# A DRAM scratch tensor laid out by token chunk instead of by channel tile, in a hybrid flow-matching step

## The chip, the cores and the metric

The kernel runs on one core of a Trainium2 chip. The metric is the device time of one execution in microseconds (us); the time of a kernel is the median of three executions. Engines are called as in the profile: PE is the matrix engine (its weight loads are PEld), DVE the vector engine, ACT the scalar engine, POOL the GpSimd engine, SP the sync engine, which here only starts DMA transfers. SPq, ACTq and POOLq are the same engines' DMA issues. On-chip memory has 128 partitions; PE writes into PSUM banks, and an engine that copies a result out of such a bank is said here to evict it.

## The reference

One layer of a network on two token groups, 2,048 sample tokens and 128 prompt tokens. The part that the change touches is the first token mixer, a gated DeltaNet: queries, keys and values come from one projection, pass a short convolution over the tokens, and are then used in 128-token chunks.

```python
proj = jnp.einsum('btd,de->bte', xn, w_in)
qkv, beta, dec, z_a, u_b, v_b, z_b, x_c, z_c, gates = jnp.split(proj, points, axis=-1)
qkv = short_conv(qkv, conv_w).astype(jnp.float32)        # 3 taps over the tokens, then SiLU
q, k, v = jnp.split(qkv, 3, axis=-1)                     # 4 heads of 128 channels each
q = l2norm(q.reshape(B, T, H_A, DK)) * (DK ** -0.5)
k = l2norm(k.reshape(B, T, H_A, DK))
o, s_f, s_b = delta_bidir(q, k, v, g, beta, s0_f, s0_b)  # chunked scan, forward and backward
o_a = (rmsnorm(o, o_norm_g) * jax.nn.silu(z_a)).reshape(B, T, W_BR)
o_b = chunk_sgu(u_b, v_b, sgu_norm_g, w_spatial, b_spatial) * jax.nn.silu(z_b)
o_c = fourier_mix(x_c, grid) * jax.nn.silu(z_c)
pb = jnp.einsum('btnw,nwd->btnd', jnp.stack([o_a, o_b, o_c], axis=2), w_branch)
merged = jnp.einsum('btnd,btnd->btd', jax.nn.sigmoid(gates), pb)
out = jnp.einsum('btd,de->bte', merged, w_out)
```

## The kernel before

Tokens stand as 17 chunks of 128: chunks 0 to 15 are the sample, chunk 16 the prompt. Every product is done in three half-precision passes (`xh`/`xl` and `whi`/`wlo` are high and low parts), so one 128-channel tile of a projection over 512 tokens is 24 matmuls.

The stages, in the order of PE's work: normalise and transpose the input, with the projection of the first gate (to about 160 us of the profile); the convolution stage (to about 430 us); the v projection of the second mixer with its spatial mixing (17 blocks of 128 tokens, to about 560 us); the rest of the second mixer, the Fourier mixer, the merges and the output projection.

The convolution stage is a loop over 12 channel tiles `ct`: tiles 0 to 3 are the four heads of q, 4 to 7 those of k, 8 to 11 those of v. For each, PE computes five token blocks (four of 512, one of 128) into PSUM banks, ACT evicts each into `raw` (L646), DVE makes the three taps into `y`, the tile `cy` (L649 to L651), ACT and POOL apply SiLU (L654, L655), POOL starts the store of the whole row to the DRAM scratch `qkvD` (L656, 128 partitions with 8.7 KB runs), and ACT takes sums of squares of q and v (L658). `raw` and `cy` have two buffers each. PSUM banks for this loop alternate between a group of three (`ps_mm`) and another three (`ps_d`).

At the end of the stage the on-chip memory of the loop (`a1p`) is given to the next tiles: the first load into it is `bsp`, the biases of the spatial mixing (L1172), and ACT's sums of squares of the v projection (L1209) write there too. So both wait for the last store of `cy`.

From there on, a second strand of work runs beside the projections: `delta()`, a Python generator that `pace.tick` and `pace.part` advance while the projections are written down, so that its instructions fall between the matmuls. Its first part, `prep`, goes over the chunks in the order 16, 0, 1, ... 15. For each it takes the four-head tiles of k, v and q from `qkvD` with `rows` (L688; tiles `kq` with three buffers for k and v, `qr` with two for q), turns them on PE (L717), normalises, splits, multiplies, and stores what the scan needs through ACT's queue (L699) and POOL's (L746, L775). After each group of four chunks, `base_inverse` loads `nd` (L804), solves on DVE (L814, L815) and hands its result `ei` to ACT's queue (two stores, L704). The scan over chunks begins at about 890 us.

SP issues nearly all loads, in one queue, in program order: weight blocks `wst` (L227), the chunk loads, the decay rows `dc` (L790), and, for the second mixer, four rows `vrow` of `vsD` (L1228, L1234), which L1240 on DVE uses. What stands in that queue behind an issue that waits, waits too. The framework's scheduler fixes the order on every engine before the run, from its own estimates of when things are ready; at run time each engine follows that order and waits on semaphores.

Of the kernel before, what the change touches and what calls it, by code (L numbers as in the profile page):

```python
# [14 lines left out]
AF = mybir.ActivationFunctionType  # L15
# [5 lines left out]
P = 128  # L21
D = 1024
KT = 8
NS = 2048
NP = 128
NTOK = NS + NP
NCH = NTOK // P
H = 4
# [10 lines left out]
TBS = [(0, 512), (512, 512), (1024, 512), (1536, 512), (2048, 128)]  # L39
# [104 lines left out]
def hybrid_flow_kernel(ctx: ExitStack, tc: tile.TileContext, x_prompt, x_sample, state_delta, c, c_ctx, ln_g, w_ada,  # L144
# [3 lines left out]
    V, A, G, PE, SY = nc.vector, nc.scalar, nc.gpsimd, nc.tensor, nc.sync  # L148
# [9 lines left out]
    def sb(pl, shape, tag, dt=F32, bufs=None):  # L158
        kw = {} if bufs is None else {"bufs": bufs}
        return pl.tile(list(shape), dt, tag=tag, name=nm(tag), **kw)  # L160
# [11 lines left out]
    def bank(pl, shape, tag="b"):  # L172
        if pl is ps_d:
            rot[0] += 1
            pl = ps_d[rot[0] % 3]
        return pl.tile(list(shape), F32, tag=tag, name=nm(tag))

    def dram(name, shape, dt=F32):
        return drp.tile(list(shape), dt, tag=name, name=name)
# [82 lines left out]
    def gemm_T(ps, w, c0, rh, rl, nkt=KT, start=True, stop=True):  # L262
        for k in range(nkt):
            mm(ps, w.hi[:, k, c0:c0 + P], rh[:, k, :], start and k == 0, False)
            mm(ps, w.hi[:, k, c0:c0 + P], rl[:, k, :], False, False)
            mm(ps, w.lo[:, k, c0:c0 + P], rh[:, k, :], False, stop and k == nkt - 1)
            if k % 2:
                pace.part(rh.shape[-1] / 400)
# [52 lines left out]
    def getw(n=1, ahead=0):  # L321
        i = wnext[0]
        wnext[0] += n
        fetch(i + n)
        while len(wdone) - len(wsteps) < i + n:
            weight_step()
        fetch(i + n + ahead)
        r = wdone[i:i + n]
        return r[0] if n == 1 else r
# [89 lines left out]
    for blk in range(8):  # L419
# [3 lines left out]
        ps = bank(ps_d, [2, 256])  # L423
# [41 lines left out]
    for ti, (t0, tn) in enumerate(TBS):  # L465
# [13 lines left out]
        for k in range(KT):  # L479
            ps = bank(ps_d, [P, tn])  # L480
            for j in range(nt):
                PE.transpose(ps[:, j * P:(j + 1) * P], xt[:, j, k * P:(k + 1) * P], ident)
            t = sb(p0p, [P, tn], "xm", bufs=3)
# [3 lines left out]
        for g in range(4):  # L487
            ps = bank(ps_d if tn == P and g % 2 else ps_mm, [P, tn])
# [15 lines left out]
    LP = NTOK + 4  # L504
# [4 lines left out]
    rq = sb(dp, [P, NCH, H], "rq")  # L509
    vqs = sb(dp, [P, 12], "vqs")  # L510
    decD = [dram(f"dec{t}", [P, 2, WB]) for t in range(NCH)]
    qkvD = dram("qkv", [12, P, LP - 2])
    dl = ExitStack()
    dq = pool(dl, "dqa", 1, side="right")
    cfs = ExitStack()
# [112 lines left out]
        flush(*last)  # L628
        yield 1

    flip = [0]
    pace.start(decays(), 1.2)
    for ct in range(12):
        w = getw(1, 2 if ct < 6 else min(4, 15 - ct))
        for half in range(1):
            raw = sb(a1p, [P, LP], "raw")
            G.memset(raw[:, 0:1], 0.0)
            G.memset(raw[:, NS + 1:NS + 3], 0.0)
            G.memset(raw[:, LP - 1:LP], 0.0)
            for t0, tn in TBS:  # L640
                flip[0] ^= 1
                ps = bank(ps_d if flip[0] else ps_mm, [P, tn])
                gemm_T(ps, w, 0, xh[:, :, t0:t0 + tn], xl[:, :, t0:t0 + tn])
                o = t0 + 1 if t0 < NS else t0 + 3
                with tc.high_priority():
                    A.activation(raw[:, o:o + tn], ps, AF.Copy, scale=w.inv)  # L646
                pace.tick(tn / 100)
            y = sb(a1p, [P, LP - 2], "cy")
            V.tensor_scalar(y, raw[:, 0:LP - 2], convw(0, ct), None, ALU.mult)  # L649
            V.scalar_tensor_tensor(y, raw[:, 1:LP - 1], convw(1, ct), y, ALU.mult, ALU.add)  # L650
            V.scalar_tensor_tensor(y, raw[:, 2:LP], convw(2, ct), y, ALU.mult, ALU.add)  # L651
            for c0 in range(0, LP - 2, CQ):
                c1 = min(c0 + CQ, LP - 2)
                A.activation(raw[:, 1 + c0:1 + c1], y[:, c0:c1], AF.Sigmoid)  # L654
                G.tensor_tensor(y[:, c0:c1], y[:, c0:c1], raw[:, 1 + c0:1 + c1], ALU.mult)  # L655
            G.dma_start(qkvD[ct], y)  # L656
            if ct < 4 or ct > 7:
                A.activation(raw[:, 1:LP - 1], y, AF.Square, accum_out=vqs[:, ct:ct + 1])  # L658
    wsn = sb(ep, [P, WB], "st", bufs=3).rearrange("p (g q) -> p g q", g=4)
    SY.dma_start(wsn, w_spatial[0].rearrange("g p q -> p g q"))  # L660
    pace.drain()
    a1.close()


# [10 lines left out]
    eD = [dram(f"ei{g}", [2, 32, len(ts), H * 512], F16) for g, ts in enumerate(GROUPS)]  # L675
    hs = lambda h: slice(h * P, (h + 1) * P)

    def chunk_off(t):
        return t * P if t < 16 else NS + 2

    def bc(col, n):
        return col.rearrange("p (h o) -> p h o", o=1).to_broadcast([P, H, n])

# [1 line left out]

    def rows(part, t):
        x = sb(d2, [P, H, P], "kq" if part else "qr", bufs=3 if part else 2)
        SY.dma_start(x, qkvD[part * 4:part * 4 + 4, :, chunk_off(t):chunk_off(t) + P].rearrange("h p t -> p h t"))  # L688
        return x

    owed = []
# [16 lines left out]
    def prep(g, ci, t, nxt, held):  # L708
# [18 lines left out]
        def more(key, make):  # L727
            if nxt is not None:
                held[key] = make()

        more(1, lambda: rows(1, nxt))
        ps = turned(1)
        norm(ps, 1)
        V.tensor_tensor(h3(tok[:, 0, :]), h3(ps), bc(ss[:, 1, :], P), ALU.mult)
        yield 1
        more(0, lambda: rows(0, nxt))
        A.activation(tok[:, 1, :], turned(2), AF.Copy, scale=us)
        norm(turned(0), 0)
# [12 lines left out]
        made = A.activation(T[:, 0, :], ps, AF.Copy, scale=FS)  # L751
        V.scalar_tensor_tensor(T[:, 1, :], ps, FS, T[:, 0, :], ALU.mult, ALU.subtract)
        more(2, lambda: rows(2, nxt))
        late([(kTD[t], T)], made)
        yield 1
# [419 lines left out]
    ps = bank(ps_x, [P, 4, P])  # L1175
# [21 lines left out]
    for t in range(NCH):  # L1197
        ps = bank(ps_mm, [P, 4, P])
# [10 lines left out]
        made = A.activation(sq, vn.rearrange("p i c -> p (i c)"), AF.Square, accum_out=ss)  # L1209
# [19 lines left out]
    for g in range(4):  # L1229
# [5 lines left out]
        for ti, (t0, tn) in enumerate(TBS):  # L1235
            st = vrow[:, t0:t0 + tn]
            ps = bank(ps_mm, [P, tn])
# [26 lines left out]
    for g in range(4):  # L1264
        xw, zw = getw(2, 2)
        for gh in range(1):
# [20 lines left out]
            for q in range(0, NCH, 4):  # L1287
                qn = min(4, NCH - q)
                ps = bank(ps_mm, [P, qn, P])
                for i in range(qn):  # L1290
                    t = q + i
# [43 lines left out]
            for q4 in range(5):  # L1335
# [8 lines left out]
                if q4 == 2:  # L1344
                    ps = bank(ps_x, [P, P])
# [182 lines left out]
    part = sb(op, [P, 3], "part", bufs=1)  # L1528
    for i_, t in enumerate(order):
# [11 lines left out]
        for i, (c0, c1) in enumerate([(0, 512), (512, 896), (896, D)] if end else [(0, 512), (512, D)]):  # L1541
            cs = slice(c0, c1)
            ps = bank(ps_mm, [P, c1 - c0])
            gemm_N(ps, mh, ml, wo, c0, c1 - c0)
            dst, gc = (hh[:, cs], gt[:, cs]) if i_ else (gp[i], gp[i])
# [52 lines left out]
```

## Time and profile before

| | us |
|---|---|
| median of three executions | 2189.1 (2187.15 to 2190.76) |
| the profiled execution's own time | 2196.42 |
| its span | 2194.6 |
| PE busy in the span | 2125.6 (97%) |
| granted PE clock | 0.99 of full speed |

The profile shows one execution. The span runs from the first to the last instruction; 1.8 us lie around it. A group's row gives the line, engine, operation and tiles, its busy time and the idle time of its engine ahead of it. In a timeline the columns are the start in us, the duration in us, the engine, the line and the operation, and in square brackets the idle time ahead and what ended it. A row of DMA issues ends with the KB of each transfer and the median us from its issue to its landing.

### The profile page before, as it was taken

Reading aid. Unit: us, or ns where it says so; the run is one execution under the profiler, and the core shown is the slowest. Engines: PE = TensorE matmul, PEld = TensorE weight load, DVE = VectorE, ACT = ScalarE, POOL = GpSimd, SP = SyncE. Lnnn points to the kernel's source line nnn. Section 1 sums busy time; section 2 is a strip of 40 time slices with the busy share of each in tenths; the row PEclk is TensorE's granted clock in tenths of the full one; section 3 lists DMA queues with packets and bytes.
Section 4 is the critical chain, followed back from the end, with each engine's and each line's share of the span. In section 5 each row is a group of like instructions: output and inputs, shape, how many; then the busy total and the mean of one; then the engine's idle time right before and its main releaser. Section 6 shows DMA issues by size and latency. Waiting matters only on the chain.

```text
span 2194.6 us, 42626 instructions
## 1 busy us (share of the span) xinstructions
PE 2125.6 (97%) x16258; PEld 1220.6 (56%) x16258; DVE 1311.4 (60%) x3141; ACT 1014.4 (46%) x2345; POOL 734.8 (33%) x893
## 2 busy tenths in 40 slices
PE   7999999999999999899899999999999999999998
PEld 3564444455555577777555555555655444444444
DVE  5736854479868697466665555665664544233454
ACT  3535644455555574444644445655553422222332
POOL 1421533223334332442322233345542222212543
PEclk9999999999999999999999999999999999999999
DMA  8424733176776653444655556766664534333542
GB/s 282 152 87 161 257 109 110 60 215 211 250 225 226 213 168 106 119 126 140 214 162 162 167 166 187 229 196 213 212 194 148 166 131 130 109 102 109 183 150 106
DMA packets 233240, 365.11 MB, mean 166 GB/s; under 512 B 38369, under 2 KB 132938, under 8 KB 230986
## 3 DMA queue, kind: packets, MB, share of 16 engines
q1 hardware_dynamic: 180650, 267.38, 39.3%
q0 software_dynamic: 12688, 51.27, 6.4%
q10 hardware_dynamic: 39696, 43.72, 5.9%
q8 instruction: 128, 2.10, 0.4%
q14 instruction: 78, 0.64, 0.1%
HBM read 234.67 MB, written 127.62 MB: 165 GB/s over the span
## 4 chain that ended last, share of the span: by engine, by line
PE 46%; DVE 7%; DMA 6%; ACT 3%; issue 2%; POOL 1%; ACTq 0%; SPq 0%; POOLq 0%; DVEq 0%
PE b L193 46%; DMA st<-br 1%; DMA wst<-in_w_blk_dram 1%; DVE XB L814 1%; DVE E L815 1%; DMA ei<-XB 1%; DMA wst<-in_w_brb_dram 1%; DVE big L1376 1%; DVE wlo L251 0%; DMA ES<-ei 0%; ACT nd L767 0%; ACT big L1375 0%; DVE sv L1002 0%; DMA of<-sz 0%; DVE o L947 0%
## 5 line engine op out<-in xcount | busy, mean ns | idle before, releaser
L193 PE MATMUL b<-xh,whi 128*128 128x512 f16 (+1 forms) x1920 | 651.4, 348 | 7.2 <-DVE sg L1152 3.7
L193 PE MATMUL b<-xl,whi 128*128 128x512 f16 (+1 forms) x1920 | 651.6, 348 | 0.0
L193 PE MATMUL b<-xh,wlo 128*128 128x512 f16 (+1 forms) x1920 | 650.6, 348 | 0.0
L193 PEld LDWEIGHTS <-whi 128*128 128x128 f16 x3904 | 357.2, 98 | 338.5 <-issue 15.1
L193 PEld LDWEIGHTS <-wlo 128*128 128x128 f16 x1952 | 191.4, 98 | 178.0 <-issue 2.1
L193 PE MATMUL b<-big,bhi 128*128 128x512 f16 (+1 forms) x960 | 251.6, 347 | 4.2 <-ACT big L1375 3.6
L1415 POOL TENSOR_TENSOR mrow<-mrow,sg 128x512 f32<-128x512 f32 (+1 forms) x80 | 94.4, 1181 | 289.8 <-DVE sg L1414 164.6
L193 PE MATMUL b<-big,blo 128*128 128x512 f16 (+1 forms) x480 | 163.4, 347 | 0.0
L1405 ACT ACTIVATE sg<-b,winv 128x512 f32<-128x512 f32 (+1 forms) x120 | 74.2, 618 | 162.0 <-PE b L193 161.6
L193 PEld LDWEIGHTS <-xh 128*128 128x128 f16 x1496 | 118.7, 99 | 35.0 <-DVE yT L1328 4.0
L655 POOL TENSOR_TENSOR cy<-cy,raw 128x545 f32<-128x545 f32 (+1 forms) x48 | 74.9, 1587 | 182.0 <-ACT raw L654 182.0
L193 PEld LDWEIGHTS <-bhi 128*128 128x128 f16 x960 | 87.2, 98 | 76.4 <-issue 1.1
L1414 DVE SCALAR_TENSOR_TENSOR sg<-b,binv,sg 128x512 f32<-128x512 f32 (+1 forms) x80 | 53.5, 668 | 104.6 <-PE b L193 96.3
L207 DVE CAST wscb<-wss 128x1 bf16<-128x1 f32 x93 | 14.3, 154 | 164.5 <-ACT wlo L241 68.2
L193 PE MATMUL b<-whi,xh 128*128 128x128 f16 x544 | 95.1, 222 | 5.7 <-DVE yT L1328 3.8
L193 PE MATMUL b<-wlo,xh 128*128 128x128 f16 x544 | 95.1, 222 | 0.0
L193 PE MATMUL b<-whi,xl 128*128 128x128 f16 x544 | 95.0, 222 | 0.0
L193 PE MATMUL b<-wohi,mh 128*128 128x512 f16 (+2 forms) x248 | 92.7, 375 | 2.1 <-ACT mh L1485 2.1
L887 POOL COPY T<-ES 32x256 f16<-32x256 f16 x68 | 30.4, 447 | 188.6 <-DMA ES<-ei 164.4
L193 PE MATMUL b<-wohi,ml 128*128 128x512 f16 (+2 forms) x248 | 92.4, 375 | 0.3 <-DVE ml L1486 0.3
L193 PE MATMUL b<-wolo,mh 128*128 128x512 f16 (+2 forms) x248 | 92.5, 374 | 0.0
L251 DVE SCALAR_TENSOR_TENSOR wlo<-wst,wsc,whi 128x1024 f16<-128x1024 f32 x52 | 72.3, 1394 | 31.3 <-ACT whi L250 30.9
(458 smaller groups left out, 4307.1 us busy)
## 6 DMA issues: line engine op xcount, KB each, us to landing
wst<-in_w_blk_dram SPq DMA_DIRECT2D x60, 512.0 KB, 5.2
qkv<-cy POOLq DMA_DIRECT2D x12, 1089.0 KB, 5.2
st<-br SPq DMA_DIRECT2D x48, 256.0 KB, 4.6
mrow<-mrg SPq DMA_DIRECT2D x18, 512.0 KB, 3.6
mrow<-mrg SPq DMA_DIRECT2D x16, 576.0 KB, 4.1
mrg<-mrow POOLq DMA_DIRECT2D x16, 576.0 KB, 3.9
dc<-dec SPq DMA_DIRECT2D x17, 512.0 KB
kq<-qkv SPq DMA_DIRECT2D x34, 256.0 KB, 5.0
```

Source lines behind the costliest of these rows:

```text
L193: PE.matmul(out, l, r, start=start, stop=stop)
L207: V.tensor_copy(sb16, ss)
L251: V.scalar_tensor_tensor(w.lo, st, s, w.hi, ALU.mult, ALU.subtract)
L655: G.tensor_tensor(y[:, c0:c1], y[:, c0:c1], raw[:, 1 + c0:1 + c1], ALU.mult)
L814: V.tensor_tensor(t3, X3[:, 0:k, k:k + 1].to_broadcast([P, k, n_]), E3[:, k:k + 1, k:32].to_broadcast([P, k, n_]), ALU.mult)
L815: V.tensor_tensor(E3[:, 0:k, k:32], E3[:, 0:k, k:32], t3, ALU.subtract)
L887: G.tensor_copy(T16[rows(a0, b), :, :, b], ES[0:32, :, 2 * a0 + b, :, wT])
L1376: V.scalar_tensor_tensor(o16[:, 1, g, t0:t0 + tn], st, s, o16[:, 0, g, t0:t0 + tn], ALU.mult, ALU.subtract)
L1405: A.activation(sg, ps, AF.Sigmoid, scale=gw.inv)
L1414: V.scalar_tensor_tensor(sg, ps, binv[:, 1:2], sg, ALU.mult, ALU.mult)
L1415: G.tensor_tensor(mr, mr, sg, ALU.add)
```

## The change

The scratch tensor's shape goes from channel tile, channel, token to token chunk, part (q, k or v), channel, head, token in the chunk. A chunk load (now L695) becomes one contiguous 256 KB block with 2 KB runs, where it was 512 runs of 512 bytes. A store of one channel tile becomes two DMAs (the function `keep`, L633): one of 128 x 16 runs of 512 bytes for the sample, one of 128 runs of 512 bytes for the prompt.

The stores also move. They were started by POOL right after its SiLU. Now a finished row waits in the list `made`, and ACT starts its two DMAs behind its eviction of the second token block of the next channel tile; the last row's two are started by SP, after `pace.drain()`. The number of DMAs for the stores goes from 12 on POOL to 22 on ACT and 2 on SP.

```diff
-    qkvD = dram("qkv", [12, P, LP - 2])
+    qkvD = dram("qkv", [NCH, 3, P, H, P])
...
-    flip = [0]
+    flip, made = [0], []
+
+    def keep(ct, y, eng):
+        dst = qkvD[:, ct // 4, :, ct % 4, :]
+        eng.dma_start(dst[0:16].rearrange("t p x -> p t x"), y[:, 0:NS].rearrange("p (t x) -> p t x", x=P))
+        eng.dma_start(dst[16], y[:, NS + 2:NS + 2 + NP])
+
     pace.start(decays(), 1.2)
...
                 with tc.high_priority():
-                    A.activation(raw[:, o:o + tn], ps, AF.Copy, scale=w.inv)
+                    ev = A.activation(raw[:, o:o + tn], ps, AF.Copy, scale=w.inv)
+                if made and t0 == TBS[1][0]:
+                    with tc.issue_after(ev.ins):
+                        keep(*made.pop(), A)
...
-            G.dma_start(qkvD[ct], y)
+            made.append((ct, y))
...
     pace.drain()
+    keep(*made.pop(), SY)
     a1.close()
...
-    def chunk_off(t):
-        return t * P if t < 16 else NS + 2
-
...
-        SY.dma_start(x, qkvD[part * 4:part * 4 + 4, :, chunk_off(t):chunk_off(t) + P].rearrange("h p t -> p h t"))
+        SY.dma_start(x, qkvD[t, part])
```

## The prediction

> **What bounds the kernel now.** I read the page's busy shares and queues first, then a table of stretches, then PE's waits, then the timelines of the queues at the places these name.
>
> ```profile
> PE 2125.6 (97%) x16258; PEld 1220.6 (56%) x16258; DVE 1311.4 (60%) x3141; ACT 1014.4 (46%) x2345; POOL 734.8 (33%) x893
> ...
> q0 software_dynamic: 12688, 51.27, 6.4%
> ```
>
> ```profile
> 190.00:430.00 240.00, 240.00 (x1322) 117.31 (x1321) 150.36 (x164) 123.94 (x176) 81.42 (x87) 1.00 0.43 152
> 440.00:900.00 460.00, 439.61 (x3592) 281.03 (x3590) 373.57 (x994) 249.92 (x738) 152.48 (x200) 0.99 0.64 196
> 443.00:450.00 7.00, 7.00 (x38) 3.67 (x37) 2.63 (x8) 2.04 (x7) 1.96 (x3) 1.00 0.90 218
> 563.00:575.00 12.00, 8.64 (x61) 5.02 (x60) 8.83 (x27) 2.80 (x5) 1.86 (x3) 1.00 1.02 346
> ```
>
> In the stretches the columns are the stretch, its length, busy time of PE, PEld, DVE, ACT, POOL, the granted clock, the DMA share and GB/s. PE is busy 2125.6 of 2194.6 us, so all idling of PE together is 69.0 us. The convolution stage has none: 240.00 of 240.00 us at clock 1.00. The stage that reads the chunks has 460 - 439.61 = 20.4 us. A change of transfers removes no matmul, so it can win only there, and can lose wherever it makes PE wait. PE's three longest waits in that stage (total, times, longest), and then two single instructions of PE with the idle time ahead of them:
>
> ```profile
> PE b L193 <- DVE sg L1152: 5.6, 3, 3.4
> PE b L193 <- DVE T L752: 3.2, 2, 2.0
> PE b L193 <- DVE vrow L1240: 2.5, 1, 2.5
> ```
>
> ```profile
> 658.84 0.59 PE L193 MATMUL b<-xh,whi 128*128 128x512 f16 x1 [3.42 <-DVE sg L1152]
> ...
> 758.31 0.63 PE L750 MATMUL b<-cst,tok 128*128 128x128 f32 x4 [1.84 <-DVE tok L734]
> ```
>
> No wait of PE names a chunk load: they arrive ahead of need. So the sum is made of a few microseconds at named places.
>
> **The price of a piece of data.** Transfers by median landing:
>
> ```profile
> qkv<-cy POOLq DMA_DIRECT2D x12, 1089.0 KB, 5.2
> ...
> kq<-qkv SPq DMA_DIRECT2D x34, 256.0 KB, 5.0
> ...
> skn<-kv SPq DMA_DIRECT2D x34, 256.0 KB, 3.1
> ...
> vs<-vs ACTq DMA_DIRECT2D x17, 256.0 KB, 4.2
> ...
> ei<-XB ACTq DMA_DIRECT2D x6, 512.0 KB, 9.5
> ```
>
> The stretch 443 to 450 us holds almost nothing but chunk loads in 512 byte runs: 0.90 x 7 us x 16 engines = 100.8 engine-us for 218 GB/s x 7 us = 1.53 MB, so 66 engine-us per MB. POOL's queue carries mostly long runs (8.7, 4 and 2 KB): 6.4% of 16 x 2194.6 us for 51.27 MB, so 44. I take 66 for 512 byte runs and 44 for 2 KB runs. A chunk load of 0.262 MB then needs (66 - 44) x 0.262 / 16 = 0.36 us less of all engines, the 51 loads 18 us less in a stage that uses 0.64 x 460 = 294 us. The stores, 13.4 MB, need 18 us more in a stage whose DMA share is 0.43.
>
> **The convolution stage: 0.** POOL loses 12 issues of 0.59 us, which nobody waited for. ACT gains 22 issues. In the order of the changed program, each pair stands behind the eviction of the second block of the next tile or a few places later, and PE's order is unchanged up to the v projection. Here are ACT's and POOL's halves of SiLU for the last tile, and two matmuls of a tile before it:
>
> ```profile
> 432.42 2.30 ACT L654 ACTIVATE raw<-cy 128x545 f32<-128x545 f32 x4 [6.66 <-DVE cy L651]
> ```
>
> ```profile
> 433.17 4.46 POOL L655 TENSOR_TENSOR cy<-cy,raw 128x545 f32<-128x545 f32 x4 [16.80 <-ACT raw L654]
> ```
>
> ```profile
> 394.64 0.38 PE L193 MATMUL b<-xh,whi 128*128 128x512 f16 x1
> 394.86 0.38 PE L193 MATMUL b<-xl,whi 128*128 128x512 f16 x1
> ```
>
> POOL ends 2.9 us after ACT (437.6 against 434.7). For q and v ACT's square already waits for that; for k it is a new wait of ACT, 2.9 us. Behind the waiting issue stand evictions, which free PSUM banks. Matmuls start 0.22 us apart, so a block of 24 takes 5.2 us and a tile 22; six banks give PE five blocks, 26 us, before it stops. An issue behind many pieces can take far longer than the usual 0.4 us. Here are ACT's issues from the second of two stores of `ei` on (2,048 pieces of 256 bytes each), and SP's in the same stretch:
>
> ```profile
> 648.72 3.42 ACTq L704 DMA_DIRECT2D ei<-XB  x1
> ...
> 652.26 3.18 ACTq L699 DMA_DIRECT2D n<-n  x1
> 655.53 1.73 ACTq L699 DMA_DIRECT2D qk<-n  x1
> 657.31 0.69 ACT L1150 ACTIVATE sg<-b,winv 128x512 f32<-128x512 f32 x1 [4.45 <-issue]
> ```
>
> ```profile
> 651.89 1.75 SPq L688 DMA_DIRECT2D kq<-qkv  x2
> ```
>
> A pair at the two worst of these costs ACT 3.42 + 3.18 = 6.6 us, with the wait 9.5, per tile of 22 us in which ACT is otherwise busy about half (123.94 of 240 us): still under 26. If that cover were gone, each pair would cost PE up to 9.5 us. The Trainium skill, "DMA: Bandwidth & Descriptors", section "Issuing engines are not separate DMA queues", says that starting DMAs on another engine saves only the issue time, which is usually small beside the transfer. The trace agrees on the usual 0.4 us and not on the 3.42; by the rule alone the third term below would be 0 and the sum a gain of 2.
>
> **The seam: +0.5.** The last row's store starts when POOL is done, before and after. Its landing releases `bsp`, and the chunk loads stand behind `bsp` in SP's queue:
>
> ```profile
> 437.93 0.59 POOL L656 DMA_DIRECT2D qkv<-cy  x1 [0.30 <-POOL cy L655]
> ```
>
> ```profile
> 442.62 0.33 SPq L1172 DMA_DIRECT2D bsp<-in_b_spatial_dram  x1
> ```
>
> ```profile
> 442.69 0.63 ACT L1209 ACTIVATE st<-sg 128x512 f32<-128x512 f32 x1 [2.91 <-DMA qkv<-cy]
> ...
> 449.59 0.72 ACT L742 ACTIVATE q<-qr,qsc 128x512 f16<-128x512 f32 x1 [4.96 <-DMA qr<-qkv]
> ```
>
> ```profile
> 449.19 1.05 PE L193 MATMUL b<-wsT,sg 128*128 128x128 f32 x8
> ...
> 450.11 1.07 PE L717 MATMUL b<-cst,kq 128*128 128x128 f32 x8
> 451.01 0.60 PE L717 MATMUL b<-cst,qr 128*128 128x128 f32 x4
> ```
>
> The median store of 1,089 KB (1.115 MB) lands in 5.2 us, of which 44 x 1.115 / 16 = 3.1 is transfer, so 2.1 is fixed. In 512 byte runs the transfer is 66 x 1.115 / 16 = 4.6; with 0.3 for the second issue it lands at 437.9 + 2.1 + 4.6 + 0.3 = 444.9, 2.3 later than 442.6. From `bsp` to the landing of q took 449.6 - 442.6 = 7.0; with three chunk loads at 0.36 less it takes 5.9, so q is there at 450.8. In the changed order the group with the turns of k, v and q stands 0.7 us of matmuls earlier, so q is wanted at 451.0 - 0.7 = 450.3: 0.5 us of waiting. ACT's square (L1209), behind the same landing, goes through POOL and DVE to PE's spatial product, which ran 6.5 us after it (449.19 against 442.69); 2.3 + 0.7 of that go, the rest hides it. Ends: 0, if the store lands as before, and, by the 9.5 us of `ei` (as many pieces, half the size, beside other traffic), a landing at 447.4, q at 453.3 and 3.0 us.
>
> **The rows of the second mixer: -2.5.** Other queues move with the schedule. SP, DVE and ACT before:
>
> ```profile
> 562.83 0.43 SPq L688 DMA_DIRECT2D qr<-qkv  x1
> 568.06 0.35 SPq L227 DMA_DIRECT2D wst<-in_w_blk_dram  x1
> 568.51 0.37 SPq L1228 DMA_DIRECT2D vrow<-vs  x1
> 568.93 0.42 SPq L1234 DMA_DIRECT2D vrow<-vs  x1
> ```
>
> ```profile
> 574.60 1.41 DVE L1240 SCALAR_TENSOR_TENSOR vrow<-b,winv,vrow 128x512 f32<-128x512 f32 x2 [0.70 <-DMA vrow<-vs]
> ```
>
> ```profile
> 562.53 0.38 ACTq L1194 DMA_DIRECT2D vs<-vs  x1
> ...
> 583.39 0.71 ACT L742 ACTIVATE q<-qr,qsc 128x512 f16<-128x512 f32 x1
> ```
>
> The rows stand behind a weight block that waited until 568 us for its buffer, so DVE had its row at 574.6 and PE lost 2.5 us (the third of its waits). In the changed order both rows stand ahead of `qr` and the weight, and the last spatial product, hence the last store of `vs`, stands about 5 us of matmuls earlier. Even if that store went at 562.5 as before, it lands 4.2 later, at 566.7, 1.8 us earlier than 568.5. With the earlier product the rows go at about 563. Both exceed, or nearly reach, the 2.5 us. `qr` and the weight now queue behind 2.2 MB, some 6 us (at the 346 GB/s of that stretch); that q is not used before 583.39, and no wait of PE there names a weight. Next late at this place is DVE with the inverse. Ends: 0 (DVE is late by itself) and -3.7 (-2.5 and the 1.2 us wait on L752 just ahead of it, 3.2 less its longest, 2.0).
>
> **ACT's blocked issues: -1.** At 658.84 and 758.31 PE lost 3.42 and 1.84 us, the first because ACT sat in the three issues shown. The chunk loads were issued into the same stretch; a chunk's three now take 3 x 0.36 = 1.1 us less. Two places, up to 1.1 each; half of it taken, since the 256 byte pieces that fill the queue stay. Ends: 0 and -5.3.
>
> **Sum.** 0 + 0.5 - 2.5 - 1 = -3 us. The profiled execution took 2196.4 (span 2194.6 and 1.8 around it), so it would take 2193.4; the median of the runs is 7.3 below that execution, so I forecast 2189.1 - 3 = 2186 us. No change from measuring is about 0.2%, 4.4 us: below 2184.7 is faster, above 2193.5 slower.
>
> **Rivals.** (1) The loads free more: all three stalls at full DMA load go, 1.2 + 2.5 + 3.42 + 1.84 = 9.0 less, with the seam 8.5 less: 2181. For it: DMA shares of 1.02 (563 to 575). Against: two of the stalls hang on `ei`, which stays as it is. (2) Slower, by the last store alone: its pieces go to 16 places 768 KB apart for each channel. If they are written at half the rate, 9.2 instead of 4.6, it lands at 449.5, q at 455.4, PE waits 5.1, and the reordered rows bring nothing because DVE, which does 373.57 of 460 us, gets its work 5 us later too: 2194. It decides when the store takes over 11 us. Against it: `vs`, in the same runs over four places, lands in 4.2. The Trainium skill, "DMA: Bandwidth & Descriptors", section "Latency and other measured facts", tells of row pitches of large powers of two in DRAM that halve the rate, 207 to 103 GB/s; ours is three times 256 KB, and no row here shows it. (3) Hidden anyway: the rows' gain is taken by the next late DVE work, and only the seam is left: 2189.6.
>
> **Chances.** Forecast 0.36 (2183 to 2189 by itself), rival 1 0.18, rival 2 0.24, rival 3 0.22. Faster: rival 1 and 0.10 of the forecast's lower end, 0.28. Slower: rival 2 nearly whole and a little for a late weight, 0.26. Same 0.46. The range goes to 2180 and 2196, into rivals 1 and 2, with about 1 in 10 outside each end.
>
> **What would show it.** PE 240 of 240 us from 190 to 430, ACT's stores at 0.4 to 3.4 us each; `bsp` at about 445, the first q turn not over 1 us late; `kq` landing in 3 to 4 us; `vrow` issued at 563 to 567 and no PE wait on L1240; PE idling of 17 to 18 us from 440 to 900. It would be wrong if evictions stall PE, if the last store takes over 11 us, if a weight behind the rows holds PE, or if the moved DVE order opens a new wait.

## The result, and the profile after

The changed kernel took 2204.42 us (median of seven, 2193.71 to 2211.59), the kernel before, on the same chip, 2190.12. The ratio is 1.0053, with a 95% interval of 1.0031 to 1.0075: slower by half a per cent. Forecast were 2186 us, in a range of 2180 to 2196: the sign was wrong, and the time lies outside the range. The profiled execution after is the longest of the seven: 2211.59 us, of which 2209.8 are span.

The page's lines of the changed kernel on the engines and on DMA queues (packets, MB, share of 16 engines), and the same queues before:

```profile
PE 2127.4 (96%) x16258; PEld 1219.8 (55%) x16258; DVE 1315.2 (60%) x3141; ACT 1013.4 (46%) x2345; POOL 722.6 (33%) x881
...
q1 hardware_dynamic: 163274, 268.49, 38.8%
...
q10 hardware_dynamic: 63984, 55.98, 7.8%
q0 software_dynamic: 10960, 37.89, 4.8%
```

```profile
q1 hardware_dynamic: 180650, 267.38, 39.3%
...
q10 hardware_dynamic: 39696, 43.72, 5.9%
```

Stretches of the changed kernel, in the columns of the prediction's table, and then one of before that was not yet shown:

```profile
160.00:450.00 290.00, 283.19 (x1706) 139.81 (x1703) 158.52 (x197) 140.41 (x202) 78.06 (x80) 0.99 0.42 134
190.00:430.00 240.00, 233.28 (x1260) 112.29 (x1258) 143.19 (x160) 122.11 (x172) 73.60 (x76) 0.99 0.47 150
450.00:910.00 460.00, 437.34 (x3536) 279.58 (x3535) 376.20 (x992) 248.52 (x738) 150.31 (x199) 0.98 0.62 195
```

```profile
160.00:450.00 290.00, 290.00 (x1742) 144.23 (x1740) 165.77 (x206) 142.47 (x209) 88.44 (x95) 1.00 0.41 141
```

The stage forecast at nothing lost 6.81 us of PE (290 - 283.19), where before it lost none. The stage in which the gain was forecast got no better. PE comes to it 9.65 us later (below), so 450 to 910 us stands against 440 to 900 us before: 460 - 437.34 = 22.7 us of idle PE, against 20.4. PE's waits from 160 to 450 us (total, times, longest) name who was late:

```profile
PE b L193 <- DVE wscb L207: 2.8, 1, 2.8
PE b L193 <- DVE wlo L251: 2.6, 2, 1.9
PE b L193 <- ACT raw L652: 1.3, 2, 1.1
```

Only 1.3 of the 6.7 us are evictions (L652). The rest is the preparation of the next weight block, which goes over three engines: ACT squares and sums it (L241), DVE narrows the sum (L207), PE multiplies that by ones to spread it over the partitions (a matmul of one column), DVE makes the scale, ACT writes the high part `whi` (L250), DVE the low part `wlo` (L251). Here is the longest of these waits on ACT, DVE and PE, in timelines of the changed kernel:

```profile
344.39 0.38 ACTq L635 DMA_DIRECT2D qkv<-cy  x1
344.81 1.65 ACTq L636 DMA_DIRECT2D qkv<-cy  x1
346.51 0.69 ACT L652 ACTIVATE raw<-b,winv 128x512 f32<-128x512 f32 x1 [4.47 <-issue]
347.10 1.14 ACT L250 ACTIVATE whi<-wst,wsc 128x1024 f16<-128x1024 f32 x1
348.13 0.93 ACT L652 ACTIVATE raw<-b,winv 128x512 f32<-128x512 f32 x2
348.95 1.06 ACT L241 ACTIVATE wlo<-wst 128x1024 f16<-128x1024 f32 x1
```

```profile
348.26 1.28 DVE L251 SCALAR_TENSOR_TENSOR wlo<-wst,wsc,whi 128x1024 f16<-128x1024 f32 x1 [8.50 <-ACT whi L250]
...
350.73 0.15 DVE L207 CAST wscb<-wss 128x1 bf16<-128x1 f32 x1
```

```profile
350.93 0.16 PE L193 MATMUL b<-wscb,ones 128*128 128x1 bf16 x1 [2.78 <-DVE wscb L207]
350.96 0.59 PE L193 MATMUL b<-xl,whi 128*128 128x512 f16 x1
351.34 0.63 PE L193 MATMUL b<-xh,wlo 128*128 128x512 f16 x1
```

And the same weight before, on DVE and on PE:

```profile
338.76 0.15 DVE L207 CAST wscb<-wss 128x1 bf16<-128x1 f32 x1
```

```profile
342.87 0.17 PE L193 MATMUL b<-wscb,ones 128*128 128x1 bf16 x1
```

The reader is to see two things. First, the tiny matmul had little slack. Before, DVE's number was ready at 338.91 and PE came for it at 342.87: 4.0 us. Afterwards PE came at 348.15 (its end of work, 350.93 - 2.78), 5.3 later than before, while DVE was ready at 350.88, 12.0 later: a relative delay of 6.7, which is the slack of 4.0 and the wait of 2.8. ACT's idle time ahead of its eviction, "4.47 <-issue", is the larger part of it. Its first half is the wait of the first issue for POOL, whose part of SiLU ends at 344.36 (row below), the second the two issues, 344.39 to 346.46.

```profile
339.90 4.46 POOL L664 TENSOR_TENSOR cy<-cy,raw 128x545 f32<-128x545 f32 x4 [13.09 <-ACT raw L663]
```

Second, the wait costs more than its length. Behind it matmuls start 0.42 us apart, where they start 0.22 apart otherwise; the granted clock in stretches of 2 us was

```profile
350.00:352.00 2.00, 1.07 (x4) 0.43 (x4) 2.00 (x3) 0.10 (x2) 0.00 (x0) 0.70 0.66 240
352.00:354.00 2.00, 2.00 (x6) 0.70 (x5) 1.41 (x2) 1.25 (x3) 0.00 (x0) 0.50 0.06 23
354.00:356.00 2.00, 2.00 (x11) 0.83 (x9) 2.00 (x2) 0.47 (x1) 0.00 (x0) 0.95 0.00 0
```

so eight matmuls took 3.3 us instead of 1.7: 1.6 us on top of the 2.8.

That adds up for this stage. PE's matmuls there stand in the same order in both kernels, so the first and the twelfth matmul of `wscb` in it mark the same work, here before and then in the changed kernel:

```profile
226.35 0.17 PE L193 MATMUL b<-wscb,ones 128*128 128x1 bf16 x1
...
413.47 0.17 PE L193 MATMUL b<-wscb,ones 128*128 128x1 bf16 x1
```

```profile
226.87 0.17 PE L193 MATMUL b<-wscb,ones 128*128 128x1 bf16 x1
...
423.12 0.17 PE L193 MATMUL b<-wscb,ones 128*128 128x1 bf16 x1
```

The lag grows from 0.5 to 9.65 us, by 9.1. PE's waits give 6.7 of it and the halved clock 1.6. The other 0.8 is the gap that each of the five waits leaves besides: a matmul of 512 columns lasts 0.38 us, but the next starts 0.22 behind it, so a stop costs 0.16 more than the idle time that is shown. Of the other 6.1 us of the 15.2 between the spans' ends (2209.8 - 2194.6), 0.5 lie ahead of the stage and 2.3 are the idle time between 450 and 910 us. The rest lies later, where the change moves nothing. Another execution of the changed kernel (e11, below) has a span of 2193.9 us, though it loses 1.6 us in the convolution stage, so I do not put these 6.1 us down to the change as a whole.

How long the issues take shows in the durations of ACT's two issues per row (minimum, median and maximum in ns):

```profile
L635 ACTq DMA_DIRECT2D qkv<-cy x11: 377/377/379, 218.7 to 425.2; - x11
```

```profile
L636 ACTq DMA_DIRECT2D qkv<-cy x11: 1242/1854/4292, 219.1 to 425.6; - x11
```

The first, of 2,048 pieces, takes 0.38 us. The second has only 128 pieces, but stands right behind the first, and holds ACT for 1.2 to 4.3 us. I call this the hold. What makes the issue take so long inside the queue is not shown.

### The profile page after: what moved, and what is told of

It is laid out like the page before. It is cut to its first block, busy times and chain, and to the rows that moved or that the text cites. A ratio compares the mean times of both kernels' runs of the same rounds, so it can differ in the third digit from the quotient of the medians.

```text
span 2209.8 us, 42645 instructions
## 1 busy us (share of the span) xinstructions
PE 2127.4 (96%) x16258; PEld 1219.8 (55%) x16258; DVE 1315.2 (60%) x3141; ACT 1013.4 (46%) x2345; POOL 722.6 (33%) x881
## 3 DMA queue, kind: packets, MB, share of 16 engines
q1 hardware_dynamic: 163274, 268.49, 38.8%
## 4 chain that ended last, share of the span: by engine, by line
PE 44%; DMA 6%; DVE 6%; ACT 2%; issue 2%; POOL 1%; SPq 0%; POOLq 0%; DVEq 0%; ACTq 0%
PE b L193 44%; DMA st<-br 2%; DMA wst<-in_w_blk_dram 1%; DMA ei<-XB 1%; DMA mt<-mrg 1%; DVE big L1383 1%; DMA wst<-in_w_brb_dram 1%; DVE XB L821 0%; DVE E L822 0%; DVE o L954 0%; DVE wlo L251 0%; ACT big L1382 0%; DMA of<-sz 0%; POOL st L1169 0%; POOL o L1075 0%
## 5 line engine op out<-in xcount | busy, mean ns | idle before, releaser
L207 DVE CAST wscb<-wss 128x1 bf16<-128x1 f32 x93 | 14.3, 154 | 158.3 <-ACT wlo L241 62.8
L251 DVE SCALAR_TENSOR_TENSOR wlo<-wst,wsc,whi 128x1024 f16<-128x1024 f32 x52 | 72.4, 1395 | 36.8 <-ACT whi L250 36.0
```

The lines of the kernel that those rows point to most:

```text
L207: V.tensor_copy(sb16, ss)
L251: V.scalar_tensor_tensor(w.lo, st, s, w.hi, ALU.mult, ALU.subtract)
```

## The experiments

The diffs are against the changed kernel, with `big` for the sample's store of 2,048 pieces and `small` for the prompt's of 128. "Idle" is PE's idle time between 160 and 450 us in the profiled execution.

**e1: the old layout at the new place.** One store per row in the layout of before (8.7 KB runs), issued by ACT behind the second block of the next tile; the chunk loads are those of before too.

```diff
-    qkvD = dram("qkv", [NCH, 3, P, H, P])
+    qkvD = dram("qkv", [12, P, LP - 2])
...
-        dst = qkvD[:, ct // 4, :, ct % 4, :]
-        eng.dma_start(dst[0:16].rearrange("t p x -> p t x"), y[:, 0:NS].rearrange("p (t x) -> p t x", x=P))
-        eng.dma_start(dst[16], y[:, NS + 2:NS + 2 + NP])
+        eng.dma_start(qkvD[ct], y)
...
```

> The old layout with the changed kernel's move alone: one store per channel tile in 8.7 KB runs, started by ACT behind the second block's eviction (the last one by SP). PE, DVE and POOL stand in exactly the order of the changed kernel. Theory A (ACT sits in the issue of the second of two DMAs, behind 2,048 short pieces, and the weight splits behind it come late): PE idles under 1 us between 160 and 440 us, ACT's issues take 0.4 us, time 2190 to 2197. Theory B (the wait of ACT for POOL is enough): PE still idles 4 us or more there, time 2197 to 2204. Theory C (the loss is in the chunk stage, from the new order): conv stage clean, yet 2200 or more.

Measured: 2197.33 against 2193.73 us, ratio 1.0016 (1.0005 to 1.0027), idle 0. The move to ACT by itself does not make PE wait. ACT's issues here took 0.33 to 0.40 us.

**e2: small first.** The two stores of a row in the other order, all else the same.

```diff
-        eng.dma_start(dst[0:16].rearrange("t p x -> p t x"), y[:, 0:NS].rearrange("p (t x) -> p t x", x=P))
         eng.dma_start(dst[16], y[:, NS + 2:NS + 2 + NP])
+        eng.dma_start(dst[0:16].rearrange("t p x -> p t x"), y[:, 0:NS].rearrange("p (t x) -> p t x", x=P))
```

> The changed kernel with the two DMAs of a store in the other order: the prompt's 128 pieces first, then the sample's 2,048. Same bytes, same places. Theory A: nothing is issued right behind the many pieces in tiles 4 to 10, so ACT is free after 0.8 us; PE idles under 2 us between 160 and 440 us (6.8 in the changed kernel's profile), time 2193 to 2199. Theory B: PE idles 4 us or more, time 2200 to 2206. Theory C: time within 3 us of the changed kernel's.

Measured: 2195.89 us, ratio 1.001 (0.9997 to 1.0023), idle 0. The same pieces and the same places; the hold is gone from the pair, as the row of its second issue shows (the first took 0.33 to 0.39 us):

```profile
L636 ACTq DMA_DIRECT2D qkv<-cy x11: 446/448/789, 218.3 to 415.5; - x11
```

It is not gone from the queue. In two early rows ACT issues a store of decay rows (`dec`) within 0.4 us of the pair, and this issue, otherwise 0.33 us, is held in its place:

```profile
238.27 1.59 ACTq L610 DMA_DIRECT2D dec<-dc  x1
...
257.96 1.91 ACTq L610 DMA_DIRECT2D dec<-XB  x1
```

**e3 and e7: one block later,** behind the eviction of the third block instead of the second, so that POOL has ended its half of SiLU more often: e3 with small first, e7 with the changed kernel's order.

```diff
-                if made and t0 == TBS[1][0]:
+                if made and t0 == TBS[2][0]:
```

> As the run with the small DMA first, but the pair stands behind the third block's eviction, so that for the k tiles POOL is done when ACT comes to it. PE, DVE, POOL and SP stand in the same order as in that run. Theory A: within 2 us of that run. Theory B: 3 us or more faster than that run, because ACT no longer waits for POOL.

> The changed kernel with its order of DMAs, the pairs of the k tiles behind the third block's eviction instead of the second's; PE, DVE, POOL and SP in exactly the changed kernel's order. Theory A with ACT's hold alone: issues of 1.2 to 4.3 us stay, PE still idles 3 us or more between 160 and 450 us, time within 4 us of the changed kernel's. If the hold harms only together with ACT's wait for POOL: the stall near 350 us (2.8 us) goes, those at 250 to 276 us stay, time 3 to 5 us less.

Measured: e3 2197.59 us, 1.0012 (0.9997 to 1.0026), the same as e2; e7 2200.65 against 2189.96, 1.005 (1.0034 to 1.0066), the same as the changed kernel. The later place changes nothing with the hold or without it. One thing did not fit: the profile of e7 (an execution of 2196.91 us) showed only 0.15 us of idle, where 3 or more were expected. That is what e12 is for.

**e4: the layout alone.** Both stores of a row issued by POOL right after SiLU, as before the change.

```diff
-                if made and t0 == TBS[1][0]:
-                    with tc.issue_after(ev.ins):
-                        keep(*made.pop(), A)
...
-            made.append((ct, y))
+            keep(ct, y, G)
...
-    keep(*made.pop(), SY)
```

> The new layout with the stores where they were, started by POOL right after its part of SiLU, two DMAs each. Theories A and B: ACT is not touched, PE idles under 1 us between 160 and 440 us, time 2186 to 2194. Theory C: time 2198 or more, from the chunk stage. A further way: POOL's issue of 2,048 pieces takes microseconds and delays SiLU, which shows as POOL time and, at the seam, as a later landing of the last row.

Measured: 2196.55 us, ratio 1.001 (1.000 to 1.002), idle 0. The time is above the 2186 to 2194 that were expected; the kernel before took 2193.73 beside it. This is the whole layout without ACT's part, and it gains nothing: what chunk loads in 2 KB runs save, less what the stores in short runs cost, is worth no time here.

**e5: the changed kernel again.**

> The changed kernel once more, beside the others of this call and with a second profile. All theories: 1.003 to 1.007 of the kernel before; PE idles 4 us or more between 160 and 450 us, at places where a weight split or a scale is late. If it idles under 1 us there and the time is as long, the stall that its first profile showed is not the cause.

Measured: 2199.38 us (2194.45 to 2206.65) against 2189.96, ratio 1.004 (1.0021 to 1.0058); idle 1.85 in an execution of 2194.45 us, its fastest. The ratio is as expected; the idle time is not, since 4 us or more were expected. e11 and e12 come back to this.

**e6: small by POOL, big by ACT.** The orders of PE and DVE are those of the changed kernel.

```diff
-        eng.dma_start(dst[16], y[:, NS + 2:NS + 2 + NP])
+        G.dma_start(dst[16], y[:, NS + 2:NS + 2 + NP])
```

> The changed kernel with the second DMA of a store (the prompt's 128 pieces) started by POOL instead of ACT. PE and DVE stand in exactly the changed kernel's order; ACT's queue differs only by the 11 missing issues. Theory A (the second issue on the same queue is what holds ACT): ACT's remaining issues take 0.4 us, PE idles under 1 us between 160 and 450 us, time 5 us or more below the changed kernel's in this call. Theory B (2,048 short pieces slow everything, whoever issues): as the changed kernel, within 3 us.

Measured: 2196.13 against 2189.96 us, ratio 1.0023 (1.0009 to 1.0037), idle 0. ACT still issues every big store, at 0.37 to 0.53 us. That is 3.2 us below e5 and 4.5 below e7, less than the 5 that were expected. So a third to two fifths of the loss of e5 and e7 goes with the issue behind the big store. The profile is of the longest of its executions, 2200.78 us, and has no idle time.

**e8: halves.** Big in two stores of 1,024 pieces, then small, all on ACT.

```diff
-        eng.dma_start(dst[0:16].rearrange("t p x -> p t x"), y[:, 0:NS].rearrange("p (t x) -> p t x", x=P))
+        for c0 in (0, 8):
+            eng.dma_start(dst[c0:c0 + 8].rearrange("t p x -> p t x"), y[:, c0 * P:(c0 + 8) * P].rearrange("p (t x) -> p t x", x=P))
```

> The price of the hold by itself: the sample's DMA cut into two of 1,024 pieces, then the prompt's 128, all on ACT. If an issue is held until the pieces of the one before it are out (about 1 ns to 2 ns per piece: 1.24 to 4.29 us behind 2,048), the second and third issues take 0.6 to 2.2 us each, and ACT is held as long in all as in the changed kernel: time within 4 us of it. If the hold comes only behind more than some number of pieces, both are at 0.4 us, and the time is that of the run with the small DMA first.

Measured: 2194.04 against 2189.96 us, ratio 1.0016 (1.000 to 1.0031), idle 0. The whole is between the two expectations: the time is that of small first, and small's issue takes a little longer than the usual 0.4 us:

```profile
L637 ACTq DMA_DIRECT2D qkv<-cy x11: 564/605/1807, 217.4 to 415.0; - x11
```

So behind 1,024 pieces issued 0.4 us earlier the hold is nearly gone. But the two halves do not stand back to back: the second goes out 1.6 to 4.2 us after the first, because it waits for POOL's later part of SiLU. Whether the hold goes by the pieces of one store or by all pieces issued shortly before, these runs do not separate.

**e9 and e10: more hold, and the same traffic without it.** A third store per row, a scratch copy of big that nobody reads, between big and small: e9 issues it from ACT, e10 from POOL. PE and DVE have the same order in both. The diff is e9's; in e10 `G` stands for `eng` in the added store.

```diff
+    copyD = dram("copy", [16, 3, P, H, P])
...
         eng.dma_start(dst[0:16].rearrange("t p x -> p t x"), y[:, 0:NS].rearrange("p (t x) -> p t x", x=P))
+        eng.dma_start(copyD[:, ct // 4, :, ct % 4, :].rearrange("t p x -> p t x"), y[:, 0:NS].rearrange("p (t x) -> p t x", x=P))
```

> The changed kernel with a third store per tile of channels: a scratch copy of the 16 sample blocks (2,048 pieces of 512 bytes), issued by ACT between the sample's store and the prompt's. So two of ACT's issues per tile stand behind 2,048 pieces instead of one (1.2 to 4.3 us each in the changed kernel's traces). Theory (the held queue of ACT makes PE wait through the weight splits behind it): hold per tile at least doubled, 4 to 9 us; PE loses 5 to 30 us of 290 between 160 and 460 us, and the ratio to the kernel before is 1.007 to 1.02. Rival (the loss comes from something else in the schedule or from the scattered pieces as traffic): as the changed kernel, 1.003 to 1.006, and no more idle time of PE in the convolution stage than e10 shows.

> The same kernel as e9 with the same order of PE's and DVE's instructions and the same bytes, only that the scratch copy is issued by POOL. Theory (the hold counts, not the traffic): ACT's issues behind 2,048 pieces stay one per tile, so the ratio is that of the changed kernel, 1.003 to 1.007, and below e9 by at least 0.003. Rival (traffic): the same as e9 within 0.002.

Measured: e9 2232.84 against 2192.92 us, ratio 1.0182 (1.0164 to 1.020); e10 2208.66, 1.0079 (1.0064 to 1.0094). Small's issue and the stretch from 160 to 450 us, e9 first:

```profile
L638 ACTq DMA_DIRECT2D qkv<-cy x11: 3366/3634/6057, 221.9 to 452.9; - x11
```

```profile
160.00:450.00 290.00, 269.79 (x1566) 131.06 (x1563) 149.76 (x184) 132.48 (x192) 66.63 (x76) 0.96 0.53 163
```

```profile
L638 ACTq DMA_DIRECT2D qkv<-cy x11: 1684/3232/6507, 218.0 to 434.1; - x11
```

```profile
160.00:450.00 290.00, 279.01 (x1641) 137.21 (x1639) 158.00 (x193) 139.72 (x202) 80.34 (x89) 0.98 0.56 172
```

In e9 the copy's own issue was held too (1.7 to 3.5 us). Idle rises from 6.8 to 20.2 us, and the granted clock falls to 0.96; between the two matmuls of `wscb` the stage is 28.3 us longer than before (table below). The same bytes issued by POOL cost 0.0103 less: the queue counts first. But e10 came out above its expectation (1.003 to 1.007), and its row says how: the median hold rose from 1.85 to 3.23 us although ACT issues no more than in the changed kernel. Other stores in flight lengthen the hold, so traffic matters through it, and idle rises to 11.0 us; the rival theory, traffic by itself, would have made e9 and e10 alike. That none of e10's loss is traffic by itself is not shown.

**e11 and e12: one more execution each** of the changed kernel and of e7's.

> The changed kernel once more, for another profiled execution. Theory: its length beyond 2190 us and the idle time of PE between 160 and 450 us go together: some 2 us idle at 2194, 7 us at 2211. Rival: the length varies for other reasons, and the idle time does not follow it.

> The kernel of e7 once more: its profile showed 0.15 us of idle PE in the convolution stage though its times lay 0.5% above before. Theory: a longer execution than that profile's shows some us of PE waits on weight splits there. Rival: no idle time in the convolution stage in a long execution either, and the loss must lie elsewhere in that kernel.

Measured: e11 2195.68 us, e12 2206.88 us. Their stretches from 160 to 450 us, e11 and then e12:

```profile
160.00:450.00 290.00, 288.59 (x1728) 142.92 (x1725) 163.03 (x206) 142.09 (x208) 69.69 (x83) 1.00 0.44 139
```

```profile
160.00:450.00 290.00, 282.86 (x1689) 139.39 (x1686) 156.86 (x197) 140.42 (x202) 78.42 (x80) 0.99 0.42 134
```

With e5, e7 and the first profile, the five executions of these two kernels fall into two groups by the idle time: 0.15, 1.41 and 1.85 us in those of 2196.91, 2195.68 and 2194.45; 6.81 and 7.14 in those of 2211.59 and 2206.88. Here is the time between the first and the twelfth matmul of `wscb` in every profile:

| profiles | executions, us | stage, us |
|---|---|---|
| before | 2196.42 | 187.1 |
| no hold in the pair: e1, e2, e3, e4, e6, e8 | 2190.94 to 2200.78 | 187.1 to 187.3 |
| hold, short: e7, e11, e5 | 2196.91, 2195.68, 2194.45 | 187.4, 188.7, 189.1 |
| hold, long: first profile, e12 | 2211.59, 2206.88 | 196.3, 196.8 |
| longer hold: e10, e9 | 2207.39, 2227.07 | 203.0, 215.4 |

The long ones do lose time there: of the 10.0 us between e7 and e12, one kernel, 9.4 are in this stage; of the 15.9 between e11 and the first profile 7.6. The wait shown above keeps its cover in the kernels without the hold: at that place DVE's number is ready ahead of PE in all six, by 4.0 us in e1 and e6, as before the change, by 1.9 in e2 and by 0.7, the least, in e3; in the first profile, e5, e11 and e12 PE waits for it.

What differs between the long and the short ones is POOL's half of SiLU for one early row. The changed kernel's first profile and e11:

```profile
227.85 12.00 POOL L664 TENSOR_TENSOR cy<-cy,raw 128x545 f32<-128x545 f32 x4 [6.84 <-ACT raw L663]
```

```profile
226.78 8.44 POOL L664 TENSOR_TENSOR cy<-cy,raw 128x545 f32<-128x545 f32 x4 [6.83 <-ACT raw L663]
```

In e12 it took 12.00 us too, in e5 and e7 9.57. Where it is late, the issue that waits for it is late, and the hold comes on top (4.29 us at 240.31 in the first profile, 2.90 in e11). Lateness alone is harmless: before the change the same four pieces took 11.99 us, and in e8 11.84, with no idle PE in either. That this row decides between long and short rests on five profiles, and why POOL needs 8.4 us in one execution and 12.0 in another was not tried.

**Together.** With the hold: 1.0053, 1.004 and 1.005, and 1.0079 and 1.0182 where it was made longer. Without it, 1.001 to 1.0023 in six kernels, with any layout, issuer and place. So 0.2 to 0.4% is the hold; measured side by side, e5 and e7 lie 3.2 to 6.6 us above e6 and e8, which is 0.15 to 0.3%. The remaining 0.1 to 0.2% is at the bound of what can be measured, and its place was not found. One candidate stands in the changed kernel and also in e1 and e6: a wait of PE of 2.0 us at a later turn of q (L724, at 614.92 us in the changed kernel) that the profile before does not have and for which the profile names no cause. None of these versions is faster than the kernel before.

## Why the prediction was wrong

**The convolution stage (forecast 0): the step that failed.** The size of the blocked issue was within its bound: 9.5 us per pair, from the issues behind `ei`, where the place shown above has 4.47. Its cover was wrong. The step says "Behind the waiting issue stand evictions, which free PSUM banks", and compares the 9.5 with the 26 us that six banks give. But ACT's queue also holds L241 and L250, the preparation of the next weights, and PE's fixed order has the matmul that spreads the sum in the middle of a tile. Its slack was 4.0 us, and could have been read in the trace of before from two rows, DVE's L207 and PE's matmul of `wscb`. With it, the step's own fallback sentence applies, that each uncovered pair costs PE up to 9.5 us: five waits of up to 2.8 us came out. The 26 us did not hold for the evictions either: in the changed kernel ACT evicted nothing from 260.5 to 271.2 us, and PE stood 1.1 us for want of it. The halved clock behind a wait was in no term.

**The price of the issue.** The usual 0.4 us was right for the first issue of a pair and wrong for the second. A long issue was taken as a worst case, from the `ei` rows; in the changed kernel a hold of 1.2 to 4.3 us stood at every pair. The Trainium skill, "DMA: Bandwidth & Descriptors", section "Issuing engines are not separate DMA queues", calls the time to initiate a DMA usually small beside the transfer. This trace agrees for the first store (0.38 us, with 5.5 from issue to landing) and not for the second, 1.2 to 4.3 us for 0.066 MB.

**The seam (forecast +0.5): a little better.** SP's queue in the changed kernel:

```profile
447.30 0.38 SPq L635 DMA_DIRECT2D qkv<-cy  x1
447.73 1.85 SPq L636 DMA_DIRECT2D qkv<-cy  x1
452.80 0.33 SPq L1179 DMA_DIRECT2D bsp<-in_b_spatial_dram  x1
```

From the last store's issue to `bsp` it is 5.5 us, against 442.62 - 437.93 = 4.7 before: 0.8 later, where 2.3 were forecast. No wait of PE stands at the first turn of q.

**The rows of the second mixer (forecast -2.5): the place was right, the gain went back into the transfer.** SP and DVE in the changed kernel:

```profile
573.87 0.32 SPq L1235 DMA_DIRECT2D vrow<-vs  x1
```

```profile
582.84 1.41 DVE L1247 SCALAR_TENSOR_TENSOR vrow<-b,winv,vrow 128x512 f32<-128x512 f32 x2 [3.04 <-DMA vrow<-vs]
```

Counted from the last row's store, the rows are issued at 126.6 us, 4.0 earlier than before (568.51 - 437.93 = 130.6), but DVE starts on them at 135.5, only 1.1 earlier than before (136.7): they took 9.0 us to DVE instead of 6.1. The DMA was no fuller meanwhile (a share of 0.95, against 0.97 before), but four loads of 256 KB stood close ahead of the rows on SP, from 571.42 us on, where before it was one weight block of 512 KB. That this made them late is not shown. PE's waits from 440 to 910 us show 3.7 us for it instead of 2.5:

```profile
PE b L193 <- DVE sg L1159: 5.8, 4, 3.4
PE b L193 <- DVE vrow L1247: 3.7, 1, 3.7
```

**ACT's blocked issues (forecast -1): nothing.** PE's waits on `sg` in that list went from 5.6 to 5.8 us.

**The price of the data: too far apart.** The landings of the chunk loads in the changed kernel are

```profile
qkv<-cy ACTq DMA_DIRECT2D x11, 1024.0 KB, 5.5
...
kq<-qkv SPq DMA_DIRECT2D x34, 256.0 KB, 5.1
...
qr<-qkv SPq DMA_DIRECT2D x17, 256.0 KB, 5.6
```

against 5.0 and 5.8: 2 KB runs land no sooner (the first line is the stores'). SP's loads on q1 went from 39.3% of 16 x 2194.6 to 38.8% of 16 x 2209.8 engine-us, which is 81 less, or about 140 with the last store's 60 taken off: 9 us of all engines, give or take 3 for the rounding, where 18 were forecast. The stores in 512 byte runs cost, by q10, 7.8% of 16 x 2209.8 less 5.9% of 16 x 2194.6 = 686 engine-us for 12.26 MB, 56 per MB and not 66; those that left q0 41, not 44.

**The rivals.** The faster one did not come: the idle time of its stage did not fall. The slower one named 2194 us by a last store of over 11 us; that store took 5, so it got the sign by a mechanism that did not occur. "Hidden anyway" was right for the layout: e4 is 0.1% slower, with no gain in all.

## What to carry to other kernels

Before a DMA issue is moved into a computing engine's queue, list everything that stands behind it there, the preparation of later operands too, and read each one's slack in the trace of before, from its last producer's row to its consumer's; the smallest of these is the cover, not the number of PSUM banks. Where two DMAs must go out together from such an engine, put the one of few pieces first, split the large one, or give the second to another queue, and look what the engine issues next: e2's decay stores took over the hold. Longer runs in a transfer brought nothing here, where no engine waited for its landing.

## What the runs showed of the hardware

A DMA issue right behind a store of 2,048 pieces on the same queue held its engine 1.2 to 4.8 us on ACT (e12 has the longest), on SP 1.85 us; with another 2,048 pieces in flight from POOL, up to 6.5. In the other order the median was 0.45 us, and 0.6 us behind two stores of 1,024 that stood apart. It need not be the same tensor: in e2 a decay store right behind was held 1.59 and 1.91 us. POOL's own issues in e4 took 1.21 us for 2,048 pieces and 0.56 for 128, without one holding the next.

A wait of PE of 2.78 us was followed by 3.3 us at half the granted clock; in e12 one of 1.94 us was too, while one of 1.91 us in the changed kernel's first profile and one of 2.43 us in e10 were not. The Trainium skill, "TensorE: Matmul & The Clock Gate", section "Part 1: The HAM clock gate", puts the fall to half rate behind a whole idle window of some 3.4 us. These rows have it behind shorter waits, and not behind every one of the same length.
